# Scores of both RWKV heads of a chunk by one matmul with 256 moving columns, masked in pieces of two chunks

## The chip, the cores and the metric

The kernel runs on one core of a Trainium2 chip. The metric is the time of one execution on the device in microseconds, the median of a few runs. Five engines with queues of their own work in parallel: PE (matmul; its weight loads are listed apart as PEld), DVE (vector), ACT (activation), POOL, and SP, which here only issues DMAs. Each engine executes its own list of instructions strictly in order, and an instruction that waits for a semaphore holds up all that stand behind it on that engine.

## The reference, cut to what matters

The program is one decoder layer for a sequence of 1024 positions at model width 1024: a mixer with three head groups (a gated unit, a linear recurrence, and six heads of RWKV-7 time mixing), and a gated feed-forward. The change touches only the RWKV-7 part:

```python
def step(state, inp):
    r_t, w_t, k_t, v_t, kk_t, a_t = inp
    sa = jnp.einsum('bhvk,bhk->bhv', state, kk_t)
    state = (state * w_t[:, :, None, :]
             - sa[..., :, None] * (kk_t * a_t)[..., None, :]
             + v_t[..., :, None] * k_t[..., None, :])
    return state, jnp.einsum('bhvk,bhk->bhv', state, r_t)
...
_, out = lax.scan(step, state0, tuple(seq_first))
```

The kernel computes this recurrence in chunks of 64 positions. Within a chunk it needs the products of every position's two queries (`kk` and `r`, scaled by the accumulated decay) with every position's two keys (`kk*a` and `k`), cut by a causal mask. These products are the scores.

## The kernel before, in words

The sequence is worked in two halves of 512 positions (f = 0 and 1), and the six heads in three pairs (j = 0, 1, 2). One call of `rwkv(j, f)` does a pair for a half; such a call is a unit below, named by its two digits, so unit 21 is j=2 of the second half. A unit has eight chunks in two groups g of four, and its pair of heads hh lies on the 128 partitions as 64 and 64.

`KB` holds the keys, [128, chunk, 2, 64]: for each chunk a stationary operand of 128 columns. `KG[g]` holds the queries, [128, chunk, 2, 128]: it is block-diagonal over the heads, so the 64 columns of head hh are zero on the partitions of the other head. The score matmuls take a chunk's `KB` as weights and, for each head, the 2x64 columns of that head in `KG` as the moving operand: 128 columns, eight matmuls for a group, four into each of two `pg` tiles (one for each head). Two DVE operations then mask each `pg`: line 633 writes the upper 64 rows times `mr` into `AK`, and line 635 writes the lower 64 rows times a causal mask into `SC`. `pg` comes from the PSUM pool `mp` with three buffers, which almost all small products of the mixer share.

What follows from them: `AK` goes to DRAM and comes back in other shapes (lines 642 to 687) for the triangular inverse, of which `lanes()` does one half on DVE (lines 678 and 680, fifteen small steps) and `chain()` the other on PE (line 695, tiles `pz`, `py`). Then `chain()` runs over the eight chunks one after the other: each step is a few matmuls (line 748, tile `q`), a copy `Y` on ACT, again a matmul, `U` on DVE (line 760), the new state `SS` on DVE (line 766), so it is a round trip over three engines; every step waits for the state of the one before. `finish()` normalises the result (lines 777 to 799). The names in these stages carry the unit: `q_217` is chunk 7 of unit 21.

The stages are generators, and the string `ORDER` says in which order they are advanced when the program is built (P is a unit's start, L its lanes, M with two digits its chain, E its finish, and R, B, U belong to the other groups). That order is only a priority: within each engine the instructions are then ordered when the program is built, by expected durations and dependencies, unless they are pinned. So an operation of another length moves its neighbours, all through the mixer. The large products (lines 251 to 253, three matmuls of 512 columns for each of eight row blocks, because each operand is split into a high part and a low part) stand between the small ones. Their low weights `wl_...` are made on DVE (line 234). After the mixer come the output projection (`po`, line 1036) and the feed-forward, from about 600 us on.

Of the kernel before, what the change touches and what calls it, by code (L numbers as in the profile page):

```python
# [10 lines left out]
F32 = mybir.dt.float32  # L11
# [3 lines left out]
ALU = mybir.AluOpType  # L15
# [3 lines left out]
P = 128  # L19
# [135 lines left out]
def trunk(ctx: ExitStack, tc: tile.TileContext, xT, wmod, w_in, w_out, w_up, w_down,  # L155
          par, const, sgu_ln, sgu_wT, sgu_b, lora, g2w, lruw, outT):
    nc = tc.nc
    V, A, G, T = (Ordered(tc, e) for e in (nc.vector, nc.scalar, nc.gpsimd, nc.tensor))
# [18 lines left out]
    m64 = cst[:, C_M64:C_M64 + P]  # L177
# [129 lines left out]
    mp = ctx.enter_context(tc.tile_pool(name="mp", bufs=3, space=PSUM))  # L307
# [182 lines left out]
    for i in range(2):  # L490
        r_, c_ = slice(64 * i, 64 * i + 64), slice(384 * i, 384 * i + 384)
# [26 lines left out]
    mr = r2.tile([P, 8, P], F32, name="mr")  # L518
    G.tensor_copy(mr[:, :, 64:P], m64[:, 64:P].unsqueeze(1).broadcast_to([P, 8, 64]))

    def t2(nm):
        return r2.tile([P, H], F32, tag="t2", name=nm, bufs=NT2)
# [29 lines left out]
    def rwkv(j, f, stages):  # L552
        jc = slice(j * P, (j + 1) * P)
        n = f"{j}{f}"
# [3 lines left out]
        KG, SC, ST = [[t[i] for i in gi] for t in (KGd, SCd, STd)]  # L558
        AK = AKd[turns["p"] % 2]
# [18 lines left out]
        a = t2(f"a{n}")  # L578
# [25 lines left out]
        KB = r2.tile([P, 8, 2, 64], F32, tag="KB", name=f"KB{n}", bufs=2)  # L604
# [17 lines left out]
        eng("rk", "G").tensor_tensor(k, r, k, ALU.mult)  # L622

        for g in range(2):
            pg = [mp.tile([P, 4, 2, 64], F32, tag="m", name=f"pg{n}{g}{hh}") for hh in range(2)]
            for hh in range(2):
                r_ = slice(64 * hh, 64 * hh + 64)
                for c in range(4):
                    T.matmul(pg[hh][:, c, :, :], KB[:, 4 * g + c, :, :].rearrange("p a b -> p (a b)"),  # L629
                             KG[g][:, c, :, r_], start=True, stop=True)  # L630
            for hh in range(2):
                r_ = slice(64 * hh, 64 * hh + 64)
                V.tensor_tensor(AK[r_, 4 * g:4 * g + 4, :, r_], pg[hh][0:64],
                                mr[r_, 4 * g:4 * g + 4, :].rearrange("p c (q t) -> p c q t", q=2), ALU.mult)
                V.tensor_tensor(SC[g][r_, :, :, r_], pg[hh][64:128],
                                m64[64:128, :].rearrange("p (q t) -> p q t", q=2).unsqueeze(1)
                                .broadcast_to([64, 4, 2, 64]), ALU.mult)

        dA = drp.tile([8, 2, 4160], F32, tag="dA", name=f"dA{n}", bufs=3)
        for hh in range(2):  # L640
            r_ = slice(64 * hh, 64 * hh + 64)
# [5 lines left out]
        for g in range(2):  # L647
# [3 lines left out]
            for q in range(2):  # L651
                for hh in range(2):
                    r_ = slice(64 * hh, 64 * hh + 64)
# [330 lines left out]
    for f in range(2):  # L984
        stages[f"X{f}"] = x_in(f)
        for j in range(3):
            stages[f"P{j}{f}"] = rwkv(j, f, stages)
            stages[f"B{j}{f}"] = lru(j, f, stages)
        stages[f"U{f}"] = sgu(f)
    V.on = VPIN > 0  # L990
    for nw, w in enumerate(ORDER.split()):
        if nw == VPIN:
            V.on = False
        n, _, c = w.partition("*")
# [309 lines left out]
    for k in range(KT):  # L1304
        n = (g1 - g0) * P
# [120 lines left out]
```

## Time and profile before

| | |
|---|---|
| median of 3 runs | 1365.76 us (1365.09 to 1372.66) |
| the profiled execution | 1365.03 us |
| its span in the profile | 1362.9 us |
| mean granted TensorE clock | 0.961 of full speed |
| PE, DVE, ACT, POOL busy | 92%, 67%, 43%, 21% of the span |

The span is what the profile covers; 2.1 us of the profiled execution lie outside it. PE is the engine that is busy most, and it is seldom idle for long; where it is, the profile says which instruction it waited for. A share is an average over the whole program: the mixer, to which the change belongs, is the first 570 us.

### The profile page before, as it was taken

How to read it: one execution, taken by the hardware profiler on the slowest of the kernel's cores; microseconds unless marked ns; L12 is line 12 of the kernel's file. 1: busy time of each engine (PE TensorE's matmuls, PEld its weight loads, DVE VectorE, ACT ScalarE, POOL GpSimd, SP SyncE). 2: the span in 40 equal slices, each digit the busy share in tenths (PEclk: the TensorE clock that was granted, in tenths of full speed). 3: DMA queues.
4: the chain of work that ended last, by engine and by line, in shares of the span. 5: the costliest groups of instructions: out<-in, count | busy, mean ns of one | idle time of the engine just before them, and what ended most of it. 6: DMA issues, size and time to landing. Idle time of an engine off the chain costs nothing. (4 is left out here: it accounts for less than half of the span.)

```text
span 1362.9 us, 18607 instructions
## 1 busy us (share of the span) xinstructions
PE 1248.6 (92%) x6948; PEld 1021.3 (75%) x6948; DVE 913.0 (67%) x1703; ACT 583.0 (43%) x1008; POOL 289.2 (21%) x258
## 2 busy tenths in 40 slices
PE   3769999879998989789988899999999999999996
PEld 3557878667786867668867788888888888888885
DVE  6878776777778586567797666666656675332566
ACT  5365554665663367234453334343343342111231
POOL 6652221304123100000002433333233200000000
PEclk9889999889999889889988899999999999999998
DMA  7444151443315144585232222222222373321213
GB/s 288 153 140 135 41 162 53 130 128 90 100 40 153 32 115 144 175 271 168 86 84 92 87 85 93 75 73 93 85 93 66 128 256 123 92 86 43 82 55 124
DMA packets 87498, 153.88 MB, mean 113 GB/s; under 512 B 37617, under 2 KB 39281, under 8 KB 87409
## 3 DMA queue, kind: packets, MB, share of 16 engines
q1 hardware_dynamic: 87264, 152.45, 35.6%
q8 instruction: 54, 0.88, 0.3%
q14 instruction: 36, 0.29, 0.1%
q10 hardware_dynamic: 144, 0.26, 0.1%
HBM read 126.60 MB, written 26.08 MB: 112 GB/s over the span
## 5 line engine op out<-in xcount | busy, mean ns | idle before, releaser
L1266 DVE SCALAR_TENSOR_TENSOR x<-pd,modc,x 128x512 f32<-128x512 f32 x80 | 59.6, 749 | 83.7 <-PE pd L253 83.7
L292 POOL TENSOR_TENSOR macc<-macc,wm 128x512 f32<-128x512 f32 x35 | 54.3, 1551 | 95.1 <-ACT wm L290 90.3
L233 ACT CAST wh_wd<-wr_wd 128x768 fp32r<-128x768 f32 (+2 forms) x32 | 21.7, 677 | 96.5 <-PE pd L252 94.2
L1207 POOL TENSOR_TENSOR wr_uv<-wr_uv 128x512 f32<-128x512 f32 x3 | 5.7, 1910 | 233.3 <-DVE wr_ub L1206 233.3
L234 DVE TENSOR_TENSOR wl_ug<-wr_ug,wh_ug 128x1024 fp32r<-128x1024 f32 x22 | 29.1, 1323 | 36.9 <-ACT wh_ug L233 36.6
L1315 POOL TENSOR_TENSOR x<-x,rb_n 128x512 f32<-128x512 f32 x2 | 3.0, 1516 | 218.5 <-ACT rb_n L275 218.5
L1244 POOL TENSOR_TENSOR u<-u,g 128x512 f32<-128x512 f32 x21 | 27.7, 1320 | 99.6 <-ACT g L1155 99.6
L233 ACT CAST wh_ug<-wr_ug 128x1024 fp32r<-128x1024 f32 x22 | 23.2, 1054 | 40.6 <-PE pA L1130 32.7
L1223 DVE TENSOR_TENSOR p<-p,pB 128x512 f32<-128x512 f32 x21 | 14.4, 686 | 32.8 <-PE pB L1131 30.4
L748 PE MATMUL q<-SS,KGd 128*128 128x64 f32 x180 | 35.6, 281 | 0.0
L768 ACT COPY O<-q 128x64 f32<-128x64 f32 x48 | 10.1, 210 | 58.3 <-PE q L748 58.2
L629 PE MATMUL pg<-KGd,KB 128*128 128x128 f32 x192 | 29.4, 300 | 5.4 <-DVE KGd L614 5.4
L748 PE MATMUL q<-VV,SCd 128*128 128x64 f32 x192 | 32.8, 278 | 1.4 <-ACT VV L662 0.8
L1148 DVE SCALAR_TENSOR_TENSOR g<-pA,pr,g 128x511 f32<-128x511 f32 (+1 forms) x42 | 31.2, 744 | 3.6 <-ACT g L1146 3.5
L748 PEld LDWEIGHTS q<-VV,SCd 128*128 128x128 f32 x192 | 28.5, 196 | 5.7 <-ACT VV L662 1.6
L1148 DVE SCALAR_TENSOR_TENSOR g<-p,pr,g 128x511 f32<-128x511 f32 (+1 forms) x42 | 32.1, 765 | 0.5 <-ACT g L1146 0.4
L1155 ACT ACTIVATE g<-g 128x512 f32<-128x512 f32 x44 | 27.9, 634 | 9.8 <-DVE g L1150 9.8
L290 ACT ACTIVATE wm<-wm,cs 128x512 f32<-128x512 f32 x35 | 24.5, 721 | 17.6 <-DMA wm<-in_wmod_dram 17.5
L760 DVE TENSOR_SCALAR U<-q,rn 128x64 f32<-128x64 f32 x48 | 13.5, 280 | 27.6 <-PE q L748 21.5
L629 PEld LDWEIGHTS pg<-KGd,KB 128*128 128x128 f32 x192 | 26.3, 209 | 6.2 <-DVE KGd L614 5.9
L233 ACT CAST wh_wo<-wr_wo 128x1024 fp32r<-128x1024 f32 x16 | 16.7, 1049 | 31.3 <-PE po L252 16.2
L1209 POOL TENSOR_TENSOR wr_ug<-wr_ug,wr_uv 128x512 f32<-128x512 f32 x18 | 28.9, 1604 | 1.4
(5029 smaller groups left out, 4415.0 us busy)
## 6 DMA issues: line engine op xcount, KB each, us to landing
wm<-in_wmod_dram SPq DMA_DIRECT2D x48, 512.0 KB, 4.6
wr_ug<-in_w_up_dram SPq DMA_DIRECT2D x22, 512.0 KB, 3.7
wr_uv<-in_w_up_dram SPq DMA_DIRECT2D x22, 512.0 KB, 3.6
wr_g<-gd SPq DMA_DIRECT2D x22, 512.0 KB, 3.5
x<-in_xT_dram SPq DMA_DIRECT2D x32, 256.0 KB, 4.8
wr_wo<-in_w_out_dram SPq DMA_DIRECT2D x16, 512.0 KB, 4.6
wr_wd<-in_w_down_dram SPq DMA_DIRECT2D x16, 384.0 KB, 3.1
gd<-c SPq DMA_DIRECT2D x21, 256.0 KB, 2.0
```

The lines of the kernel that those rows point to most:

```text
L233: A.copy(hi, src)
L234: (e or V).tensor_tensor(lo, src, hi.bitcast(F32), ALU.subtract)
L290: A.activation(acc if k == 0 else wt[:, j, :], wt[:, j, :], AF.Copy, scale=cs[:, k:k + 1])
L292: G.tensor_tensor(acc, acc, wt[:, j, :], ALU.add)
L629: T.matmul(pg[hh][:, c, :, :], KB[:, 4 * g + c, :, :].rearrange("p a b -> p (a b)"), KG[g][:, c, :, r_], start=True, stop=True)
L748: T.matmul(o, w, x, start=start, stop=True, skip_group_check=True)
L1148: V.scalar_tensor_tensor(g[:, d:H], src[:, 0:H - d], taps[2 - d], g[:, d:H], ALU.mult, ALU.add)
L1155: A.activation(g, g, AF.Silu)
L1209: eng("S4" + e, "G").tensor_tensor(g1, g1, v1, ALU.subtract)
L1223: V.tensor_tensor(self.p1, self.p1, psB, ALU.add)
L1244: eng("c22", "V").tensor_tensor(u3, u3, g1_, ALU.mult)
L1266: V.scalar_tensor_tensor(x, ps, modc[:, 40 + k:41 + k], x, ALU.mult, ALU.add)
```

## The change

Both heads of a chunk are now scored by one matmul: `KG[g][:, c, :, :]` is the moving operand, all 256 columns, so a group has four matmuls instead of eight. A `pg` tile holds two chunks with both heads instead of four chunks with one; its size is the same, and there are still two for a group. A mask operation reads one head's columns of two chunks, so a group has eight operations of 64x256 elements instead of four of 64x512.

```diff
--- before.py
+++ after.py
@@ -622,19 +622,19 @@
         eng("rk", "G").tensor_tensor(k, r, k, ALU.mult)
 
         for g in range(2):
-            pg = [mp.tile([P, 4, 2, 64], F32, tag="m", name=f"pg{n}{g}{hh}") for hh in range(2)]
-            for hh in range(2):
-                r_ = slice(64 * hh, 64 * hh + 64)
-                for c in range(4):
-                    T.matmul(pg[hh][:, c, :, :], KB[:, 4 * g + c, :, :].rearrange("p a b -> p (a b)"),
-                             KG[g][:, c, :, r_], start=True, stop=True)
-            for hh in range(2):
-                r_ = slice(64 * hh, 64 * hh + 64)
-                V.tensor_tensor(AK[r_, 4 * g:4 * g + 4, :, r_], pg[hh][0:64],
-                                mr[r_, 4 * g:4 * g + 4, :].rearrange("p c (q t) -> p c q t", q=2), ALU.mult)
-                V.tensor_tensor(SC[g][r_, :, :, r_], pg[hh][64:128],
-                                m64[64:128, :].rearrange("p (q t) -> p q t", q=2).unsqueeze(1)
-                                .broadcast_to([64, 4, 2, 64]), ALU.mult)
+            pg = [mp.tile([P, 2, 2, P], F32, tag="m", name=f"pg{n}{g}{i}") for i in range(2)]
+            for c in range(4):
+                T.matmul(pg[c // 2][:, c % 2, :, :], KB[:, 4 * g + c, :, :].rearrange("p a b -> p (a b)"),
+                         KG[g][:, c, :, :], start=True, stop=True)
+            for i in range(2):
+                cg = slice(4 * g + 2 * i, 4 * g + 2 * i + 2)
+                for hh in range(2):
+                    r_ = slice(64 * hh, 64 * hh + 64)
+                    V.tensor_tensor(AK[r_, cg, :, r_], pg[i][0:64, :, :, r_],
+                                    mr[r_, cg, :].rearrange("p c (q t) -> p c q t", q=2), ALU.mult)
+                    V.tensor_tensor(SC[g][r_, 2 * i:2 * i + 2, :, r_], pg[i][64:128, :, :, r_],
+                                    m64[64:128, :].rearrange("p (q t) -> p q t", q=2).unsqueeze(1)
+                                    .broadcast_to([64, 2, 2, 64]), ALU.mult)
 
         dA = drp.tile([8, 2, 4160], F32, tag="dA", name=f"dA{n}", bufs=3)
         for hh in range(2):
```

The matmuls with tile `pg` fall from 96 to 48 and the masks rise from 48 to 96; all else is the same work. The order on the engines changes through the mixer, down to the first rows of the output projection; the feed-forward's order is unchanged. Three places follow.

DVE, in unit 20, ahead of `wl_yg20`, the low weights of the gate product of R20 (`LX20`, `LT20` are the steps of unit 20's lanes, `rsq_o10` belongs to the finish of unit 10, `ig10` and `xr10` to the linear recurrence). Before:

```order
L680 TENSOR_TENSOR LX20_2219<-LX20_2219,LT20_2220 128x4x8
L225 TENSOR_TENSOR rsq_o10_2269<-rsq_o10_2269 128x8
L816 SCALAR_TENSOR_TENSOR xr20_2346<-pb20_2321,pr_66,xr20_2346 128x509
L678 TENSOR_TENSOR LT20_2220<-LX20_2219,LA20_2218 128x35
L226 SCALAR_TENSOR_TENSOR rsq_o10_2269<-rsq_o10_2269 128x8
L845 TENSOR_TENSOR ig10_1666<-ig10_1666,xr10_1659 128x512
L680 TENSOR_TENSOR LX20_2219<-LX20_2219,LT20_2220 128x5x7
L224 TENSOR_TENSOR rsq_o10_2269<-rsq_o10_2269 128x8
L846 SCALAR_TENSOR_TENSOR xr10_1659<-rg10_1665,ig10_1666 128x512
L678 TENSOR_TENSOR LT20_2220<-LX20_2219,LA20_2218 128x30
L225 TENSOR_TENSOR rsq_o10_2269<-rsq_o10_2269 128x8
L234 TENSOR_TENSOR wl_yg20_2421<-wr_yg20_2420,wh_yg20_2422 128x1024
```

After:

```order
L838 SCALAR_TENSOR_TENSOR rg10_1665<-ig10_1666,rg10_1665 128x512
L678 TENSOR_TENSOR LT20_2220<-LX20_2219,LA20_2218 128x14
L782 TENSOR_SCALAR mv10_2261<-mv10_2261 128x8
L840 SCALAR_TENSOR_TENSOR ig10_1666<-rg10_1665 128x512
L680 TENSOR_TENSOR LX20_2219<-LX20_2219,LT20_2220 128x14
L220 TENSOR_SCALAR rsq_o10_2269<-mv10_2261 128x8
L222 TENSOR_SCALAR rsq_o10_2269<-mv10_2261 128x8
L678 TENSOR_TENSOR LT20_2220<-LX20_2219,LA20_2218 128x26
L221 TENSOR_SCALAR rsq_o10_2269<-rsq_o10_2269 128x8
L234 TENSOR_TENSOR wl_yg20_2421<-wr_yg20_2420,wh_yg20_2422 128x1024
```

`wl_yg20` now stands ahead of `ig10` and `xr10` (845, 846) and of seven pairs of lane steps.

PE, at the start of unit 11's chain over the chunks (`q_110`, `q_111`), with `pb21`, a large product of the linear recurrence. Before:

```order
L253 MATMUL pb21_4514<-h14h_2658,wl_xr21_4509 128x512
L748 MATMUL q_110_4066<-Y110_4067,AKd0_121 128x64
L748 MATMUL q_110_4066<-SS_98,KGd2_114 128x64
L251 MATMUL pb21_4514<-h15h_2665,wh_xr21_4510 128x512
L252 MATMUL pb21_4514<-h15l_2666,wh_xr21_4510 128x512
L253 MATMUL pb21_4514<-h15h_2665,wl_xr21_4509 128x512
L748 MATMUL q_110_4066<-U110_4068,STd2_120 128x64
L251 MATMUL pb21_4514<-h16h_2672,wh_xr21_4510 128x512
L252 MATMUL pb21_4514<-h16l_2673,wh_xr21_4510 128x512
L253 MATMUL pb21_4514<-h16h_2672,wl_xr21_4509 128x512
L748 MATMUL q_110_4066<-U110_4068,AKd0_121 128x64
L748 MATMUL q_111_4081<-SS_98,KGd2_114 128x64
```

After:

```order
L253 MATMUL pb21_4514<-h17h_2679,wl_xr21_4509 128x512
L748 MATMUL q_110_4066<-Y110_4067,AKd0_121 128x64
L748 MATMUL q_110_4066<-SS_98,KGd2_114 128x64
L748 MATMUL q_110_4066<-U110_4068,STd2_120 128x64
L748 MATMUL q_110_4066<-U110_4068,AKd0_121 128x64
L748 MATMUL q_111_4081<-SS_98,KGd2_114 128x64
L748 MATMUL q_112_4096<-VV11_3407,SCd2_117 128x64
L748 MATMUL q_111_4081<-Y111_4082,AKd0_121 128x64
```

The large matmuls of `pb21` that stood inside the chain's first steps now stand ahead of the chain.

PE, at the end of the last chain, unit 21, and ahead of its finish (`po21`); `po02` is the third tile of the output projection. Before, from the chain's last matmul on (three more rows of `po02` and then `po21` follow):

```order
L748 MATMUL q_217_4919<-U217_4921,AKd1_122 128x64
L252 MATMUL po02_5151<-y03l_5045,wh_wo02_5147 128x512
L253 MATMUL po02_5151<-y03h_5044,wl_wo02_5146 128x512
L251 MATMUL po02_5151<-y04h_5050,wh_wo02_5147 128x512
L252 MATMUL po02_5151<-y04l_5051,wh_wo02_5147 128x512
L253 MATMUL po02_5151<-y04h_5050,wl_wo02_5146 128x512
L251 MATMUL po02_5151<-y05h_5054,wh_wo02_5147 128x512
L252 MATMUL po02_5151<-y05l_5055,wh_wo02_5147 128x512
L253 MATMUL po02_5151<-y05h_5054,wl_wo02_5146 128x512
L251 MATMUL po02_5151<-y06h_5060,wh_wo02_5147 128x512
L252 MATMUL po02_5151<-y06l_5061,wh_wo02_5147 128x512
L253 MATMUL po02_5151<-y06h_5060,wl_wo02_5146 128x512
```

After:

```order
L748 MATMUL q_217_4919<-U217_4921,AKd1_122 128x64
L251 MATMUL po02_5151<-y07h_5064,wh_wo02_5147 128x512
L252 MATMUL po02_5151<-y07l_5065,wh_wo02_5147 128x512
L253 MATMUL po02_5151<-y07h_5064,wl_wo02_5146 128x512
L788 MATMUL po21_5002<-ident_68,O21_4127 128x128 x4
L798 MATMUL pgt21_5013<-sgg1_2685,g2s_517 128x512
```

Of the rows of `po02`, 14 stood between the chain's last matmul and `po21`; now three do.

## Rows read from the trace of the kernel before

**Rows 1.** Windows: stretch, length, busy PE, PEld, DVE, ACT, POOL; clock; DMA.

```profile
240.00:290.00 50.00, 37.02 (x326) 27.03 (x326) 37.95 (x90) 37.48 (x63) 12.23 (x10) 0.86 0.52 148
...
440.00:490.00 50.00, 49.10 (x449) 41.53 (x449) 29.84 (x62) 21.13 (x51) 5.40 (x5) 0.90 0.23 57
...
670.00:1180.00 510.00, 497.09 (x2145) 406.93 (x2144) 337.45 (x502) 198.45 (x322) 133.29 (x96) 0.98 0.32 101
```

**Rows 2.** Instructions of tile pg: durations min/median/max in ns, first and last start.

```profile
L629 PE MATMUL pg<-KGd,KB x192: 270/275/582, 90.5 to 478.8; 128*128 128x128 f32 x192
L633 DVE TENSOR_TENSOR AKd<-pg,mr x24: 672/683/685, 92.7 to 480.5; 64x512 f32<-64x512 f32 x24
L635 DVE TENSOR_TENSOR SCd<-pg,cst x24: 692/694/697, 93.4 to 481.2; 64x512 f32<-64x512 f32 x24
```

**Rows 3.** PE timeline: start, length of the run, line, form, count.

```profile
458.87 0.61 PE L748 MATMUL q<-VV,SCd 128*128 128x64 f32 x4
...
477.26 1.78 PE L629 MATMUL pg<-KGd,KB 128*128 128x128 f32 x14
...
486.41 1.08 PE L827 MATMUL pra<-xr,lrw 128*128 128x512 f32 x2
487.33 1.02 PE L830 MATMUL pix<-xr,lrw 128*128 128x512 f32 x2
```

**Rows 4.** DVE operations on 256 elements and lane steps L678, columns as in rows 2.

```profile
L614 DVE TENSOR_TENSOR KGd<-r,gm x24: 407/423/1494, 89.0 to 473.5; 64x256 f32<-64x256 f32 x24
...
L678 DVE TENSOR_TENSOR LT<-LX,LA x90: 155/182/1300, 111.1 to 507.3; 128x30 f32<-128x30 f32 x18, 128x14 f32<-128x14 f32 x12, 128x24 f32<-128x24 f32 x12, 128x15 f32<-128x15 f32 x6
...
L900 DVE TENSOR_SCALAR sv<-pzt,smv,rsq_a x8: 535/540/543, 130.6 to 423.8; 128x256 f32<-128x256 f32 x8
```

**Rows 5.** DVE timeline: start, length; unit 20's stretch; unit 21's first and last mask.

```profile
249.49 0.68 DVE L777 TENSOR_REDUCE mv<-O 128x8 f32<-128x512 f32 x1
...
260.40 0.68 DVE L845 TENSOR_TENSOR ig<-ig,xr 128x512 f32<-128x512 f32 x1
...
261.19 1.22 DVE L846 TENSOR_TENSOR_SCAN xr<-rg,ig 128x512 f32<-128x512 f32 x1
...
262.48 1.22 DVE L234 TENSOR_TENSOR wl_yg<-wr_yg,wh_yg 128x1024 fp32r<-128x1024 f32 x1
...
476.02 0.68 DVE L633 TENSOR_TENSOR AKd<-pg,mr 64x512 f32<-64x512 f32 x1
...
481.23 0.69 DVE L635 TENSOR_TENSOR SCd<-pg,cst 64x512 f32<-64x512 f32 x1
```

**Rows 6.** PE timeline, the longest waits of the mixer; in brackets idle before, releaser.

```profile
263.75 0.80 PE L253 MATMUL pyg<-h00h,wl_yg 128*128 128x512 f32 x1 [5.79 <-DVE wl_yg L234]
...
280.21 1.05 PE L695 MATMUL pz<-X,AKd 16*32 16x16 f32 x64 [5.04 <-DVE X L700]
...
282.87 0.79 PE L251 MATMUL pc_xwa<-h10h,wh_xwa 128*128 128x512 f32 x1 [0.39 <-ACT h10h L329]
...
498.79 0.79 PE L253 MATMUL pu<-h10h,wl_u 128*128 128x512 f32 x1 [5.43 <-DVE wl_u L234]
```

**Rows 7.** Chain that ended last: start, share of one large matmul, line.

```profile
757.36 0.43 PE pD L1130
...
761.32 0.23 PE pC L1129
```

**Rows 8.** PE timeline, unit 11's chain: Y of chunks 0, 1 and 2.

```profile
455.29 0.33 PE L748 MATMUL q<-Y,AKd 128*128 128x64 f32 x2
...
458.48 0.33 PE L748 MATMUL q<-Y,AKd 128*128 128x64 f32 x2
...
461.62 0.39 PE L748 MATMUL q<-Y,AKd 128*128 128x64 f32 x2
```

**Rows 9.** PE timeline, end of the last chain and start of its finish.

```profile
555.58 0.33 PE L748 MATMUL q<-U,AKd 128*128 128x64 f32 x2
...
563.49 1.12 PE L788 MATMUL po<-ident,O 128*128 128x128 f32 x4 [4.31 <-DVE O L785]
```

## The prediction

> **What bounds the kernel now.** I read the page's busy shares first, which stand in the table above: PE 92%, DVE 67%. Matmul records overlap, so a busy PE is not yet a full one. The windows by stage come next [rows 1]. In the feed-forward (670 to 1180 us) PE is busy 497 of 510 us, and the change leaves that order alone, so nothing is won or lost there. The mixer is uneven: from 240 to 290 us PE is busy only 37 of 50 us at a clock of 0.86, while DVE is busy 38; from 440 to 490 us PE is busy 49 and DVE 30. So PE's work sets the pace in most of the mixer, and for the rest it is what PE waits for. The waits of over 5 us [rows 6] are three: at 263.75 us for `wl_yg`, at 280.21 us for `X` and at 498.79 us for `wl_u`. All three were released by DVE. So a saving on PE counts almost in full, an added wait behind DVE counts, and DVE's own time counts only where PE waits for it. A large matmul of 512 columns takes 0.43 us of the chain that ended last in one place and 0.23 us in another [rows 7]; those are TensorE's two levels, 1.2 and 2.4 GHz, and a stretch with long waits runs partly at the lower one, as the clock of 0.86 says.
>
> **Part 1, the matmuls on PE: about nothing.** A matmul on f32 data is two instructions in the trace, so 96 matmuls are 192 instructions [rows 2]. Their duration (275 ns) holds the pipeline's length; what counts is the spacing. The run of 14 takes 1.78 us in all, so a spacing is (1.78 - 0.275)/13 = 0.116 us [rows 3]. For 64 columns the run of four gives (0.61 - 0.275)/3 = 0.112 us [rows 3], the same, so below 128 columns something else than columns sets the spacing. For 512 columns, two instructions start 487.33 - 486.41 = 0.92 us before the next pair, or 0.46 us each [rows 3]. Between 0.116 us at 128 and 0.46 us at 512, a straight line gives 0.116 + 128 x 0.344/384 = 0.231 us at 256. A group then costs 8 x 0.231 = 1.85 us, where it was 16 x 0.116 = 1.86 us. So 128 columns are just the width at which the columns begin to count, and halving the number of matmuls gives nothing back. The lower bound is a 256-column instruction at the price of a 128-column one: 8 x 0.116 = 0.93 us saved for each of 12 groups, 11.1 us. I take the line, since its two ends are this kernel's own f32 matmuls, and book 0 us.
>
> The Trainium skill ("TensorE: Matmul & The Clock Gate", section "Back-to-back issue gap") speaks for the lower end: in a stream of weight loads and matmuls it gives about 81 ns for a matmul at 128 columns and 131 ns at 512. By that a group would fall from 16 x 81 = 1.30 us to at most 8 x 131 = 1.05 us, as an estimate from that page at least 3 us over the 12 groups. The trace disagrees with its size here: 0.46 us against 0.116 us is a ratio of 4, not 1.6.
>
> **Part 2, the masks on DVE: 8.6 us more work, of which I book 2.9.** Eight masks of a unit stand in sequence; in unit 21 the first starts at 476.02 us and the last at 481.23 us [rows 5], with one small operation between; their mean duration is 0.689 us [rows 2] and with the step between two it is about 0.72 us, so 8 x 0.72 = 5.8 us. There will be 16 masks of 256 elements. No row shows such a mask from PSUM. The nearest are the `KG` products, a tensor-tensor operation with 64x256 elements, 0.423 us, and line 900, which reads 256 elements from PSUM but takes two scalars by pointer, 0.540 us [rows 4]. With 0.03 us between two, the 16 take 7.2 us or 9.1 us, so a unit pays 1.4 us or 3.4 us more. Nothing makes it less than the fastest `KG` product, 0.407 us [rows 4], or 1.2 us for a unit; a gain is excluded, because the elements are the same and the operations are twice as many. I take 0.423 us, since the mask is the same kind of operation with the same shape. Six units give 8.6 us. Behind the masks stand, on DVE, the chain's `U` and `SS`, which PE waits for, and low weights. In stretches like 440 to 490 us DVE is idle for 40% [rows 1] and the delay is absorbed there; where DVE is already late [rows 6] all of it shows. I book a third, 2.9 us; the bounds are 0 and 8.6 us. The masks can also begin no earlier: the first two chunks cost PE 4 x 0.231 = 0.92 us, as the first head's four did (8 x 0.116). The DMA of `AK` follows the last masks and so is up to 1.4 us later; in the unit of [rows 6] it meets `X`, which is counted with the next part.
>
> **Part 3, the order of the neighbours: about +1 us.** Three places from the order, priced by rows.
>
> Place 1, `wl_yg20` [rows 5, 6]. From L777 at 249.49 us to the end of `wl_yg` at 262.48 + 1.22 = 263.70 us DVE needs 14.2 us. In the new order 845, 846 and seven pairs of lane steps stand behind it: 845 takes 0.68 us, 846 1.22 us [rows 5], and a lane step 0.18 us by the median of L678 [rows 4], so seven pairs 2.5 us; together 4.4 us. So the wait of 5.79 us may shrink to about 1 us, and the matmuls behind it may keep their full clock: 13 of them at 0.23 instead of 0.43 us [rows 7], 2.6 us. That is 7 us at best. Against it, the finish of unit 10 (`po10`) still needs those DVE steps, and the `h` tiles of the second half, the first of which PE takes at 282.87 us [rows 6], wait for DVE and ACT work that stands behind the finish; also the masks come later. I book -3 us, bounds -7 and 0.
>
> Place 2, unit 11's chain [rows 8]. A step over a chunk takes 458.48 - 455.29 = 3.2 us with nine large matmuls inside and 461.62 - 458.48 = 3.1 us without: it is a round trip, and the large matmuls ride in it free. Nine of them now stand ahead of the chain, at 0.23 us each [rows 7]: +2.1 us, bounds 0 (the chain may have waited anyway) and 3.
>
> Place 3, the end of the mixer [rows 9]. From the chain's last matmul at 555.58 us to `po21` at 563.49 us there are 7.9 us of round trip, of which 4.31 us are idle and 14 large matmuls fill most of the rest. Eleven of these 14 now stand ahead of the chain's end, 11 x 0.23 = 2.5 us less cover; low weights that stood inside the finish on DVE now stand where DVE waits for ACT, which I put at about 0.7 us back. I book +1.8 us, bounds 0 and 2.5.
>
> The wait at 498.79 us stays: the rows of the recurrence that leave its front are matched by large matmuls that left PE's side.
>
> **Sum.** 0 + 2.9 - 3 + 2.1 + 1.8 = +3.8 us on the profiled execution of 1365.03 us, so 1368.8 us. That execution lies 0.7 us below the median of 1365.76 us. I forecast 1369 us: no difference to speak of, a shade slower. About 1%, 13.7 us, is what a measurement of this kernel can tell from no change.
>
> **Rivals.**
>
> *Wide matmuls are cheap or place 1 pays in full.* If 256 columns cost PE what 128 do, 11.1 us go: 1358 us. If place 1 gives its 7 us and the masks stay hidden, -7 + 2.1 + 1.8 = -3.1: 1362 us. For it: PE waits little otherwise, so what is saved there counts. Against it: the 512-column rows [rows 3], and the work behind place 1. Chance 0.2 for both; only both together, with places 2 and 3 absorbed (1365 - 11.1 - 7 = 1347 us), pass 1%.
>
> *The masks are dear and DVE becomes the bound.* If 256 elements from PSUM with a strided read cost what line 900 does [rows 4], a unit pays 3.4 us, and if every unit's delay lands in front of low weights or `U` that PE waits for, as in [rows 6], that is 20 us, and with places 1 to 3 at +0.9 us the time is 1387 us. It decides from a mask of about 0.50 us: 16 x 0.53 - 5.8 = 2.7 us for a unit, 16 us in all. For it: the waits over 5 us are all behind DVE. Against: DVE is idle 40% of a stretch with masks. Chance 0.09.
>
> *The matmuls are not what the change moves at all.* PE and DVE both absorb it and the new order evens out: 1365 to 1366 us. It lies inside the forecast's range.
>
> **How the numbers follow.** The forecast with its neighbourhood (1364 to 1375 us) has 0.6, the first rival 0.2, the second 0.09, and what I have not traced in the new order, such as other neighbours moved by a few us either way, the rest. The terms' own bounds, without the rivals, reach from -7 us to 8.6 + 3 + 2.5 = +14.1 us, 1359 to 1380 us beside the median, and that is the range; it takes in most of the first rival and leaves out the second. Faster by over 1%: 0.03. Within 1%: 0.88. Slower by over 1%: 0.09.
>
> **What would show it.** In the new profile: 96 matmul instructions for `pg` at a spacing of 0.21 to 0.24 us; 96 masks at 0.41 to 0.43 us; DVE's busy time up by about 6 to 9 us, PE's sum nearly unchanged; the wait for `wl_yg` much shorter than 5.79 us, with a longer wait soon after it; a longer wait at `po21` than 4.31 us; the stretch after 670 us as long as before. The forecast is wrong if the spacing at 256 columns is nearer 0.12 us, if a mask takes over 0.5 us, or if a wait of several us appears at a place that I did not look at.

## The result and the profile after

The changed kernel takes 1389.85 us (median of 4 runs, 1387.82 to 1394.44); the kernel before took 1368.33 us on the same chip (4 runs, 1365.09 to 1372.66). The ratio is 1.0173 [1.0147, 1.0199]: 1.7% slower, where 1369 us with a range of 1359 to 1380 us was forecast. The profiled execution took 1394.44 us with a span of 1392.3 us. It is the slowest of its four, and the profile of before (1365.03 us) lies below all four runs of its kernel, so the two traces lie 29 us apart where the medians lie 21.5 us apart. Differences between traces are read with that in mind, and ratios of many runs decide.

These are the page's busy shares, first of before, then of the changed kernel:

```profile
PE 1248.6 (92%) x6948; PEld 1021.3 (75%) x6948; DVE 913.0 (67%) x1703; ACT 583.0 (43%) x1008; POOL 289.2 (21%) x258
...
PE 1270.8 (91%) x6852; PEld 1031.7 (74%) x6852; DVE 918.0 (66%) x1751; ACT 585.8 (42%) x1009; POOL 281.9 (20%) x258
```

DVE is busy only 5 us longer. PE is busy 22.2 us longer with 96 instructions fewer, and idle 7.2 us longer (its span less its busy time, 121.5 us against 114.3): most of the 29 us is PE taking longer over its own instructions, at a mean granted clock of 0.942 where it was 0.961. Whether that clock is the cause is asked below. Next the tile `pg` after, in the columns of [rows 2]:

```profile
L627 PE MATMUL pg<-KGd,KB x96: 379/380/793, 90.9 to 495.1; 128*128 128x256 f32 x96
L633 DVE TENSOR_TENSOR AKd<-pg,mr x48: 403/417/419, 93.1 to 498.6; 64x256 f32<-64x256 f32 x48
L635 DVE TENSOR_TENSOR SCd<-pg,cst x48: 425/427/429, 93.5 to 499.1; 64x256 f32<-64x256 f32 x48
```

And one group on PE's timeline (start, length of the run), four wide matmuls in eight instructions:

```profile
162.76 1.95 PE L627 MATMUL pg<-KGd,KB 128*128 128x256 f32 x8
```

The eight run in 1.95 us, so a spacing is (1.95 - 0.38)/7 = 0.224 us, against 0.231 us on the prediction's straight line between 128 and 512 columns. A group of sixteen narrow ones cost 16 x 0.116 = 1.86 us, one of eight wide ones 8 x 0.224 = 1.79 us. The masks take 0.417 and 0.427 us, against 0.423 us. The operations that the change touches cost what was forecast. By the Trainium skill ("TensorE: Matmul & The Clock Gate", section "Back-to-back issue gap") the eight would take at most 8 x 131 = 1050 ns, an estimate from its figure for 512 columns; by this row these f32 instructions of 256 columns are dearer.

Now the windows by stage that answer to [rows 1], with the end of the mixer as a fourth (500 to 600 us; the last line is the same stretch before):

```profile
240.00:290.00 50.00, 39.25 (x177) 29.12 (x176) 38.53 (x98) 37.53 (x60) 12.15 (x10) 0.88 0.55 156
440.00:490.00 50.00, 45.65 (x370) 37.56 (x368) 28.03 (x68) 15.07 (x31) 7.27 (x6) 0.80 0.22 68
500.00:600.00 100.00, 83.30 (x553) 63.39 (x551) 55.16 (x142) 52.60 (x93) 0.00 (x0) 0.80 0.38 115
670.00:1180.00 510.00, 496.29 (x2156) 406.53 (x2156) 345.12 (x522) 203.67 (x328) 133.26 (x96) 0.98 0.32 102
...
500.00:600.00 100.00, 87.47 (x592) 68.34 (x591) 63.34 (x129) 46.57 (x80) 0.00 (x0) 0.89 0.57 184
```

The feed-forward (670 to 1180 us) is as before. From 440 to 490 us PE is busy 45.65 us at a clock of 0.80, where it was 49.10 us at 0.90. From 500 to 600 us the clock is 0.80; it was 0.89. The new order is late by then, so these two stretches do not hold quite the same instructions as before. The loss lies in the mixer. In a kernel below that has the new order alone, equal instructions are late by some 7 us at 200 us, 12 us at 350, 16 us at 460 to 500 and 23 us from 600 on.

PE's waits between 60 and 690 us, by who ended them (us in total, times, longest):

```profile
PE po L788 <- DVE O L785: 6.7, 2, 6.1
PE pc_xwa L251 <- ACT h10h L329: 5.3, 1, 5.3
PE pu L251 <- ACT wh_u L233: 4.9, 1, 4.9
...
PE po L788 <- DVE LX L680: 3.0, 1, 3.0
...
PE pyg L253 <- DVE wl_yg L234: 1.0, 1, 1.0
```

Of the long waits of [rows 6] the one for `wl_yg` shrank from 5.79 to 1.0 us as forecast, and others took its place within 20 us: `po10` waits 3.0 us and `pc_xwa` 5.3 us for `h10h`. The wait of 5.04 us for `X` is gone. `po21` waits 6.1 us where it waited 4.31 us [rows 9]. But PE's idle time in this stretch, 630 us less its busy time, is 65.4 us by the windows, against 60.3 us before. Five microseconds of waits don't make 21.

### The profile page after: what moved, and what is told of

It is laid out like the page before. It is cut to its first block, busy times and chain, and to the rows that moved or that the text cites. A ratio compares the mean times of both kernels' runs of the same rounds, so it can differ in the third digit from the quotient of the medians.

```text
span 1392.3 us, 18461 instructions
## 1 busy us (share of the span) xinstructions
PE 1270.8 (91%) x6852; PEld 1031.7 (74%) x6852; DVE 918.0 (66%) x1751; ACT 585.8 (42%) x1009; POOL 281.9 (20%) x258
## 5 line engine op out<-in xcount | busy, mean ns | idle before, releaser
L292 POOL TENSOR_TENSOR macc<-macc,wm 128x512 f32<-128x512 f32 x35 | 49.4, 1413 | 76.4 <-ACT wm L290 66.0
L1244 POOL TENSOR_TENSOR u<-u,g 128x512 f32<-128x512 f32 x21 | 27.7, 1320 | 99.1 <-ACT g L1155 99.1
L233 ACT CAST wh_ug<-wr_ug 128x1024 fp32r<-128x1024 f32 x22 | 23.1, 1050 | 40.7 <-PE pA L1130 32.7
L627 PE MATMUL pg<-KGd,KB 128*128 128x256 f32 x96 | 32.1, 466 | 7.1 <-DVE KGd L614 7.1
L748 PE MATMUL q<-SS,KGd 128*128 128x64 f32 x180 | 38.6, 300 | 0.0
L748 PEld LDWEIGHTS q<-SS,KGd 128*128 128x128 f32 x180 | 31.1, 216 | 0.1
```

What stands on the lines that cost most here:

```text
L233: A.copy(hi, src)
L292: G.tensor_tensor(acc, acc, wt[:, j, :], ALU.add)
L627: T.matmul(pg[c // 2][:, c % 2, :, :], KB[:, 4 * g + c, :, :].rearrange("p a b -> p (a b)"), KG[g][:, c, :, :], start=True, stop=True)
L748: T.matmul(o, w, x, start=start, stop=True, skip_group_check=True)
```

## The experiments

### Work or order

The change does two things at once: it alters 144 operations, and it makes the build put all instructions of the mixer in another order. These kernels separate the two. Each carries a table that fixes the order of every engine's instructions, by edges that force an order and add no wait:

```diff
+PINNED = {"PE": "0-111 120-130 112-115 ...", "DVE": ..., "Activation": ..., "Pool": ..., "SP": ...}
+def pin(tc):
+    ...
+        for p, q in zip(rank, rank[1:]):
+            tc.add_manual_dep(ins[q], ins[p].name, mybir.DependencyInfo(
+                mybir.DependencyClass.NoSync, mybir.DependencyReason.DATA), reason="pin")
```

`new_work_old_order` has the changed matmuls and masks in the order of before.

> The changed kernel with every engine's instructions held in the order of the kernel before: four wide matmuls stand where the eight narrow ones stood (each in the place of the second of a pair), two half masks where one mask stood; nothing else differs. Theory A (the loss of 24 us comes from the new order of the neighbours, through waits and TensorE's half clock): 1362 to 1373 us, within 5 us of the kernel before, and the stretches at half clock as before. Theory B (the doubled masks on DVE make it late): 1380 to 1392 us. Theory C (the wide matmuls themselves are slow or let the clock fall): 1380 to 1392 us too; the run half_masks_old_order tells B from C.

Measured: 1370.28 us, ratio 0.9988 [0.9968, 1.0008].

`old_work_new_order` has the matmuls and masks of before in the changed kernel's order.

> The kernel before with every engine's instructions held in the order of the changed kernel: eight narrow matmuls stand where four wide ones stood, one mask where two half masks stood. Theory A (new order): 1382 to 1394 us, as slow as the changed kernel, with the long stretch at half clock near 540 to 570 us. Theories B and C (new work): 1360 to 1372 us.

Measured: 1392.76 us, ratio 1.0151 [1.0118, 1.0185].

`half_masks_old_order` has the narrow matmuls and the sixteen half masks, in the order of before:

```diff
             for c in range(4):
-                T.matmul(pg[c // 2][:, c % 2, :, :], KB[...], KG[g][:, c, :, :], ...)
+                for hh in range(2):
+                    r_ = slice(64 * hh, 64 * hh + 64)
+                    T.matmul(pg[c // 2][:, c % 2, :, r_], KB[...], KG[g][:, c, :, r_], ...)
```

> Narrow matmuls as before (eight in a group, 128 columns), written into tiles of two chunks, and 16 half masks in a unit as in the changed kernel, all in the order of the kernel before. Theory A: within 5 us of the kernel before, and DVE's busy time up by about 8 us. Theory B (masks): 1380 to 1392 us. Theory C (wide matmuls): as the kernel before. Its difference from new_work_old_order is the price of the matmuls' width: 0 by the prediction's line between 128 and 512 columns, -11 us by the lower bound.

Measured: 1371.18 us, ratio 1.0007 [0.9984, 1.0030].

`changed_again` is the changed kernel itself, beside the three.

> The changed kernel on the same chip as the three others, for comparison: 1386 to 1394 us, 1.5 to 2.0% over the kernel before, by every theory.

Measured: 1393.19 us, ratio 1.0147 [1.0115, 1.0179].

What follows: the order alone, with none of the changed work, costs all of it, 1.51% of 1370 us or 20.7 us. The table that fixes an order adds nothing: `changed_again` has none and takes 1.0147. The changed work in the old order costs nothing that can be measured. Between the first and the third, wide against narrow matmuls is 0.9988 against 1.0007, some 2.6 us in the wide ones' favour, less than the intervals tell; the sixteen half masks cost 1 us at 1.0007, also within them.

### Is it the half clock behind the waits?

In the new order PE's mean clock from 60 to 690 us is 0.91, before 0.94. One theory was that the waits themselves cost little, but drop TensorE to its lower level (1.2 GHz) for what follows. Zero matmuls of 512 columns, which add nothing to the sums, were put into the waits.

`new_order_waits_filled` is the changed kernel with 23 of them in six waits:

```diff
+COVER = {"pz10": 2, "po10": 3, "pc_xwa1": 5, "pu01": 5, "pz21": 2, "po21": 6}
+    def cover(ps, n, first=True):
+        zero = m64[:, 0:1].broadcast_to([P, H])
+        for _ in range(n):
+            T.matmul(ps, ident, zero, start=first, stop=False, skip_group_check=True)
```

> The changed kernel in its own order, with 23 extra matmuls of zeros (512 columns, f32, about 0.92 us each at full clock, 21 us together) put on TensorE directly ahead of six of its waits: 2 ahead of pz10, 3 ahead of po10, 5 ahead of the first of pc_xwa1, 5 ahead of pu01, 2 ahead of pz21, 6 ahead of po21. They add zeros or are overwritten. Theory A1 (the waits are short; what costs is the half clock that follows them): 1370 to 1383 us against about 1391 without them, and the time at half clock up to 660 us falls from 116 to 135 us to under 100. Theory A2 (the round trips behind DVE and ACT themselves make the loss, the clock follows from something else): 1387 to 1396 us, as without them or a little more.

Measured: 1387.62 us, ratio 1.0140 [1.0116, 1.0165].

`old_order_waits_filled` has the changed work in the order of before, with 20 of them in four of its five longest waits (`pz20`, `po21`, `pyg20`, `pu01`).

> The new work in the order of the kernel before, with 20 extra matmuls of zeros inside its own four longest waits: 6 at wl_yg20 and 5 at wl_u01 (in the middle of their groups), 5 ahead of pz20, 4 ahead of po21. Without them this kernel took 0.9988 of the kernel before. A1: 0.990 to 0.996 of the kernel before, because the stretches at half clock after 262, 280 and 497 us go. A2: 0.998 to 1.003.

Measured: 1370.07 us, ratio 1.0026 [1.0011, 1.0041].

The windows from 60 to 690 us, of the changed kernel run again and then with its waits filled:

```profile
60.00:690.00 630.00, 566.70 (x3801) 450.94 (x3801) 442.16 (x1029) 323.04 (x587) 109.23 (x124) 0.91 0.40 119
...
60.00:690.00 630.00, 580.61 (x3881) 456.77 (x3880) 445.23 (x1037) 326.99 (x595) 107.69 (x123) 0.94 0.39 118
```

The clock came back to 0.94, the level of before (over the whole program the mean is 0.954 to 0.960 in the six runs of this kernel and 0.943 to 0.948 in those of `changed_again`), and the time did not follow: 1.0140 against 1.0147. That alone decides little, because the zero matmuls are work of PE too: 23 x 0.92 = 21 us, an estimate from the f32 pair of 512 columns in [rows 3]. Their price could hide a gain from the clock. The starts of equal instructions speak against that. These are the first of `pc_xwa` and that of `po21`, each without and with the fill (the filled kernel's lines are numbered a little higher):

```profile
291.90 0.80 PE L251 MATMUL pc_xwa<-h10h,wh_xwa 128*128 128x512 f32 x1 [5.33 <-ACT h10h L329]
...
284.03 0.50 PE L259 MATMUL pc_xwa<-h10h,wh_xwa 128*128 128x512 f32 x1 [1.70 <-ACT h10h L339]
...
591.99 1.11 PE L788 MATMUL po<-ident,O 128*128 128x128 f32 x4 [6.08 <-DVE O L785]
...
584.61 0.66 PE L800 MATMUL po<-ident,O 128*128 128x128 f32 x4 [0.90 <-DVE O L796]
```

The filled kernel's trace, the fastest of its six and from another chip, lies 4.6 us ahead of the other just before its first zero matmul, and some 3 us come on behind that fill, at `pz10`. From there the lead stays: 7.7 us before the fill at `po10`, 7.9 us at `pc_xwa`, 7.4 us at `po21` and 7.8 us behind it. In between it gained 1.6 us behind `pu01` and lost 1.4 at `pz21`. As the cause of the whole loss the theory falls: behind five of the six waits the faster PE gains nothing that lasts, because it waits again for DVE and ACT (behind `pc_xwa` 1.6 us for `h10l`, where it was 0.9). At `pz21` the fill did not keep the clock up, and what the half clock costs there is seen below. In the order of before the same filling made nothing faster: 1.0026 [1.0011, 1.0041], where the same kernel without it had 0.9988.

### Where in the program

Here the order is changed over from one to the other at a point of time, on all five engines at once; what had started by then in the trace stands in the first order, the rest in the second. All have the work of before.

`new_to_305`: the new order up to 305 us.

> The work of the kernel before; every engine follows the new order as far as it had come at 305 us of the run old_work_new_order, and the old order from there. If the loss is the sum of independent places, what the new order had lost by then stays and nothing is added: 8 to 12 us over the kernel before, 1376 to 1382 us. If one late place makes the loss (pz21 with the half clock after 541 us): within 4 us of the kernel before. If a delay early on starts all the later ones: 1385 us or more.

Measured: 1376.44 us, ratio 1.0066 [1.0043, 1.0088]. In its trace `wl_u`'s matmul, at 498.79 us before [rows 6], starts at 512.65 us:

```profile
512.65 0.80 PE L253 MATMUL pu<-h10h,wl_u 128*128 128x512 f32 x1 [5.42 <-DVE wl_u L234]
```

Equal instructions from 300 to 580 us, by the median of every 20 us, are late by the same 13.8 to 14.0 us: what was lost ahead of the change-over is neither made up nor enlarged behind it. Some 3 us come back at the end of the mixer.

`old_to_500`: the order of before up to 500 us, then the new one.

> The work of the kernel before; the old order as far as it had come at 500 us of the kernel before, the new one from there. Sum of independent places: 4 to 9 us over the kernel before (the shift grows from 17 to 23 us behind 500 us in old_work_new_order). If one late place makes the whole loss: 18 to 24 us over. If the late loss only follows from an early delay: within 3 us.

Measured: 1375.85 us, ratio 1.0057 [1.0035, 1.0079].

`new_to_500`: the new order up to 500 us, then that of before.

> The work of the kernel before; the new order as far as it had come at 500 us of old_work_new_order, the old order from there: the counterpart of old_to_500, which lost 0.0057. If the stretches add, this one loses the rest of the 0.0151, 0.008 to 0.011 (1377 to 1382 us beside 1367); new_to_305 had 0.0066 of it. If the end of the mixer absorbs what was lost before: under 0.006. If the late loss needs the early one: over 0.012.

Measured: 1382.27 us, ratio 1.0111 [1.0089, 1.0134].

The stretches have 0.66% up to 305 us, 1.11 - 0.66 = 0.45% from there to 500 us, and 1.51 - 1.11 = 0.40% behind 500 us. These three add up to 1.51% by the way they are reckoned; what tests it is the last stretch taken alone, 0.57% [0.35, 0.79], which agrees with 0.40% within the intervals. So no single place holds it all.

### Single instructions put back

The next kernels take the new order with the work of before and put back what looked like the cause at one place each.

`sqrt_back`: at unit 00 the new order puts a square root, which brings two loads of ACT's function tables with it, ahead of the copies `Z` in the inverse. It goes back to where it stood:

```diff
 L233 CAST wh_u_1553<-wr_u_1551 128x1024
-L843 ACT_TABLE_LOAD
-L843 ACTIVATE ig_878<-ig_878 128x512
 L725 COPY Z_1020<-py_1097 32x256
```

> The kernel before in the new order (1.0151 of the kernel before), with two instructions put back: ScalarE's square root on ig00 (line 843) stands behind unit 10's sg and gm again, ahead of line 844, and VectorE's line 845 directly ahead of line 846. In the new order the square root stood ahead of unit 00's Z and unit 10's sg and brought two table loads of 1.28 us with it: 3.2 us for sg, and the first U of unit 00 stands behind it on VectorE. Theory D (single instructions on the path of a unit's chain, each place by itself): first U of unit 00 3 us earlier, 1.012 to 1.0135 of the kernel before. Theory E (the mixer absorbs a single place, the loss is of the order as a whole): 1.0145 to 1.0165.

Measured: 1388.65 us, ratio 1.0168 [1.0143, 1.0193].

`la_ahead`: unit 01's load of `LA` goes ahead of a load of `wm` in SP's queue.

```diff
 L642 DMA dA_2954<-AKd_122 64x8x64 x2
+L673 DMA LA_3059<-dA_2954 64x16x16 x2
 L286 DMA wm_3_3590<-in_wmod_dram 128x1024
-L673 DMA LA_3059<-dA_2954 64x16x16 x2
```

> The new order with the load of LA01 put ahead of the load of wm7_3 in SyncE's queue again, and ScalarE's square for unit 20's finish (osq20) ahead of its scaling of wm7_3. In the new order wm7_3 waited for a buffer until 354.8 us and LA01 behind it came at 355.6 us, 8 us behind the last mask of unit 01 instead of 3 us. D: unit 01's lane steps begin 4 us earlier, 1.011 to 1.013. E: 1.0145 to 1.0165.

Measured: 1385.65 us, ratio 1.0156 [1.0124, 1.0187].

`lanes_ahead`: in unit 21 the last lane steps go ahead of `o11` and its neighbours on DVE, `X` ahead of the low halves `y00l` to `y05l`, and `pz21` back between the large matmuls of `pyg21` on PE.

```diff
 L678 TENSOR_TENSOR LT_4416<-LX_4415,LA_4414 128x24
-L796 TENSOR_TENSOR o_4498<-o_4498,bv_3409 128x512
 L680 TENSOR_TENSOR LX_4415<-LX_4415,LT_4416 128x6x4
...
+L700 STREAM_TRANSPOSE X_4642<-AKd_122 32x256 x4
 L234 TENSOR_TENSOR y00l<-yr_5028,y00h 128x512
```

> The new order with unit 21's way to its chain put back: VectorE's last eight lane steps ahead of the product o11 (line 796, which waits for ScalarE) and its four transposes X121 ahead of the y lows, ScalarE's Z21 and AKd1 copies among the y casts, TensorE's pz21 in two groups ahead of the last nine and the last six matmuls of pyg21. D: first U of unit 21 5 to 6 us earlier, no half clock of 10 us and more behind 541 us, 1.010 to 1.012. E: 1.0145 to 1.0165.

Measured: 1390.6 us, ratio 1.0177 [1.0150, 1.0205].

`three_back`: all three.

> All three repairs together. D: 3 + 4 + 5.5 us less than the new order, 1.005 to 1.008 of the kernel before. E: 1.013 to 1.0165. In between: the places overlap.

Measured: 1398.91 us, ratio 1.0233 [1.0205, 1.0261].

None gave anything back, and the three together cost more than the new order alone. The traces told why the obvious edit missed its place: in `lanes_ahead` the lanes' result was ready at 523.1 us, but its DMA started at 527.13 us, behind others in SP's queue. So these followed, which mend more engines at the same places.

`unit00_back`: `sqrt_back`, and the second group of `py00` on PE back ahead of eight large matmuls.

> As sqrt_back, and TensorE's second group of py00 also stands ahead of eight large matmuls of pc_v10 again, as in the old order: all three engines on unit 00's way to its chain are put back, not ScalarE and VectorE alone (there the first U of unit 00 came only 1 us earlier, since TensorE reached py00 no sooner). Theory F (a place is worth its microseconds only if every engine and queue on the way is put back): first U of unit 00 at about 145 us, 3 us earlier, 1.012 to 1.0135 of the kernel before. Theory E (a single place is absorbed by the next one): 1.0145 to 1.017.

Measured: 1387.35 us, ratio 1.0147 [1.0123, 1.0171].

`unit21_back`: `lanes_ahead`, and SP's queue at that place as before.

> As lanes_ahead, and SyncE's queue is put back too: the two stores of LX21 ahead of the store of xr11, the two loads of AKd1 between the stores of o11 and ya01, yr02 behind them. In lanes_ahead the store of LX21 waited 4 us in the queue behind yr02 and gave the 4.6 us gain of the lane steps back. F: X121 at about 530 us instead of 534 to 536, first U of unit 21 5 to 6 us earlier, 1.010 to 1.012. E: 1.0145 to 1.017.

Measured: 1388.57 us, ratio 1.0158 [1.0128, 1.0188].

`units_back`: both.

> unit00_back and unit21_back together. F: 8 to 9 us less than the new order, 1.0075 to 1.010. E: 1.013 to 1.017.

Measured: 1392.28 us, ratio 1.0189 [1.0163, 1.0215].

Again nothing. In `unit21_back` `pz21` no longer waits, but the first `U` of unit 21 still comes only at 554.63 us. Ahead of the next step, `py`, PE now waits for the weights of the output projection, which ACT and DVE make behind the `y` halves:

```profile
542.88 0.50 PE L251 MATMUL po<-y00h,wh_wo 128*128 128x512 f32 x1 [4.66 <-ACT wh_wo L233]
```

Here a place mended by hand passed its gain on to the next instruction that was still in the new order.

### One place exchanged whole

The last two take the change-over in time again, now at both ends of one place: all that the order has between about 500 us and the first chain step of unit 21, on all five engines. The core of the edit on PE (before is -, the new order +; `wo` are the weights of the output projection):

```diff
-L695 MATMUL pz_4648<-X_4642,AKd_122 32x16 x32
 L251 MATMUL pyg_4941<-h15h,wh_yg_4937 128x512
 L252 MATMUL pyg_4941<-h15l,wh_yg_4937 128x512
 L253 MATMUL pyg_4941<-h15h,wl_yg_4936 128x512
-L695 MATMUL pz_4648<-AKd_122,Z_4643 16x16 x32
...
-L695 MATMUL py_4720<-X_4642,AKd_122 32x32 x16
...
+L695 MATMUL pz_4648<-X_4642,AKd_122 32x16 x32
+L695 MATMUL pz_4648<-AKd_122,Z_4643 16x16 x32
 L251 MATMUL po_5076<-y00h,wh_wo_5072 128x512
...
+L695 MATMUL py_4720<-X_4642,AKd_122 32x32 x16
```

`only_unit21`: the order of before everywhere, the new one at this place alone.

> Work of before. Its order of before on every engine except one place: the instructions that the new order puts between about 500 us and unit 21's first chain step (U of chunk 0) stand in the new order, all engines together; after them the order of before again. Before, the whole new order after 500 us alone cost 0.57%. If the place around unit 21's lanes, its pz and py groups and the first weights of the output projection carries that stretch's loss: 1.004 to 1.006 of the kernel before, some 6 to 8 us. If the loss is of the order as a whole, and a single place's delay is taken up at the next wait: 0.999 to 1.002.

Measured: 1375.46 us, ratio 1.0068 [1.0042, 1.0094].

`all_but_unit21`: the new order everywhere but at this place.

> The counterpart: work of before in the new order everywhere, except that the instructions between about 500 us and unit 21's first chain step stand in the order of before, all engines together. The new order up to 500 us with the order of before behind it gave 1.0111, the new order throughout 1.0151. If the place carries the last stretch's loss: 1.010 to 1.012. If the delay comes back at the next wait, as it did in the repairs of single instructions: 1.014 to 1.017.

Measured: 1379.65 us, ratio 1.0100 [1.0081, 1.0118].

Both ways the place carries the loss of its stretch: 0.68% or 9.3 us put in, 1.51 - 1.00 = 0.5% or 7 us taken out; the intervals of 1.0151 and 1.0100 meet only at their ends, at 1.0118. The rows show how. The first PE row of `wl_u` (498.79 us before) is a mark ahead of the place, and the first `U` of unit 21 one behind it. Before, rows of PE (the small matmuls `pz`, `py` with large ones between them) and the first two `U` on DVE:

```profile
518.45 0.72 PE L695 MATMUL pz<-X,AKd 16*32 16x16 f32 x64 [0.16 <-PE pyg L253]
519.10 0.50 PE L251 MATMUL pyg<-h15h,wh_yg 128*128 128x512 f32 x1
...
522.38 0.69 PE L695 MATMUL py<-X,AKd 32*32 32x32 f32 x32
...
528.69 0.28 DVE L760 TENSOR_SCALAR U<-q,rn 128x64 f32<-128x64 f32 x1 [2.46 <-PE q L748]
533.60 0.28 DVE L760 TENSOR_SCALAR U<-q,rn 128x64 f32<-128x64 f32 x1 [1.76 <-PE q L748]
```

The same of `only_unit21`:

```profile
503.77 0.80 PE L253 MATMUL pu<-h10h,wl_u 128*128 128x512 f32 x1 [5.42 <-DVE wl_u L234]
...
525.70 0.72 PE L695 MATMUL pz<-X,AKd 16*32 16x16 f32 x64 [1.65 <-DVE X L700]
526.89 0.69 PE L695 MATMUL pz<-AKd,Z 32*16 32x16 f32 x64 [0.48 <-ACT Z L707]
528.61 0.80 PE L251 MATMUL po<-y00h,wh_wo 128*128 128x512 f32 x1 [1.03 <-ACT wh_wo L233]
...
531.44 1.07 PE L695 MATMUL py<-X,AKd 32*32 32x32 f32 x32
...
540.93 0.28 DVE L760 TENSOR_SCALAR U<-q,rn 128x64 f32<-128x64 f32 x1 [9.05 <-PE q L748]
549.89 0.28 DVE L760 TENSOR_SCALAR U<-q,rn 128x64 f32<-128x64 f32 x1 [3.90 <-PE q L748]
```

And of `all_but_unit21`:

```profile
514.53 0.79 PE L253 MATMUL pu<-h10h,wl_u 128*128 128x512 f32 x1 [5.68 <-DVE wl_u L234]
...
533.97 0.72 PE L695 MATMUL pz<-X,AKd 16*32 16x16 f32 x64 [0.16 <-PE pyg L253]
...
544.21 0.28 DVE L760 TENSOR_SCALAR U<-q,rn 128x64 f32<-128x64 f32 x1 [2.46 <-PE q L748]
```

From the mark to the first `U` it is 29.9 us before, 29.7 us in `all_but_unit21`, and 37.2 us in `only_unit21` (37.2 us in `old_work_new_order` too). Of these 7.3 us, 4.1 have been lost when `py` starts (522.38 - 498.79 = 23.6 us behind the mark before, 531.44 - 503.77 = 27.7 now): `pz` waits for `X`, which stands behind six `y` halves on DVE, and `py` stands behind five large matmuls of the output projection, the first of which waits for its weights. The other 3.2 us are lost between `py` and `U` (6.3 us before, 9.5 now; 8.5 in `old_work_new_order`), and there PE waits for nothing and has fewer large matmuls than before, seven instead of ten. The windows of `only_unit21` show what it is:

```profile
510.00:520.00 10.00, 10.00 (x56) 8.02 (x55) 6.46 (x19) 5.36 (x8) 0.00 (x0) 1.00 0.58 192
520.00:530.00 10.00, 6.81 (x149) 4.87 (x147) 8.30 (x14) 6.78 (x14) 0.00 (x0) 0.88 0.66 207
530.00:540.00 10.00, 10.00 (x81) 5.51 (x82) 1.81 (x3) 6.46 (x10) 0.00 (x0) 0.50 0.42 138
540.00:550.00 10.00, 10.00 (x42) 8.43 (x42) 2.90 (x8) 3.06 (x6) 0.00 (x0) 0.50 0.07 26
```

From 524 to 529 us PE has only the small `pz` matmuls and three waits, so that it is busy 6.81 of the 10 us; then the granted clock is 0.50, the lower of the two levels, while PE is busy all the time. Before, with `pyg` between the small matmuls, the same stretch ran at 1.00:

```profile
520.00:530.00 10.00, 9.88 (x168) 6.41 (x167) 5.75 (x10) 9.48 (x18) 0.00 (x0) 1.00 0.70 220
530.00:540.00 10.00, 9.62 (x63) 8.58 (x64) 3.94 (x11) 7.45 (x13) 0.00 (x0) 1.00 0.07 27
```

How long the half clock lasts differs between runs. In `only_unit21` and the profiled run of the changed kernel it is 15.6 and 16.3 us from the first to the third `U`, in `old_work_new_order` and `changed_again` 9.9 us, before 9.5 us: another 6 us, in some profiles. The profile of `only_unit21` is the slowest of its six runs, so the traced loss of this kernel is larger than its median shows.

## Why the prediction was wrong, point by point

**What bounds the kernel: one wait was missed.** The waits of over 5 us were four, not three. The fourth stands directly ahead of the first changed matmuls:

```profile
90.50 5.18 PE L629 MATMUL pg<-KGd,KB 128*128 128x128 f32 x24 [5.21 <-DVE KGd L614]
```

After the change it is 6.6 us; nothing in the sum hung on it.

**Part 1, the matmuls: right.** The spacing is 0.224 us against 0.231, and the changed work in the old order measures 0.9988.

**Part 2, the masks: right in price; how much of it shows is too little to tell.** A mask takes 0.417 to 0.427 us against 0.423. Of the 8.6 us, 2.9 were booked as showing; the half masks alone measure 1.0007, about 1 us, and 0 and 2.9 both lie in the interval.

**Part 3, the order of the neighbours, is the step that failed.** It was entered at about +1 us, from three places priced one by one, with every other neighbour that the new order moves put at nothing and no row to say why. It is +20.7 us. None of the three places brings that, nor all of them. Place 1 happened as described: the wait for `wl_yg` went from 5.79 to 1.0 us. It returned nothing that lasts, since the next instructions of the finish (`po10`, 3.0 us) and the `h` tiles (`h10h`, 5.3 us) came late, the very counter-argument that was named and then booked at less than the gain. The wait for `X`, which part 2 passed on to this part, was priced nowhere; it went away. Place 2 was booked at 2.1 us with a bound of 3; from the first to the last `U` of unit 11's chain the traces show 30.8 us before (456.01 to 486.83 us) and 35.6 us after (468.46 to 504.04 us), 4.8 us more:

```profile
456.01 0.26 DVE L760 TENSOR_SCALAR U<-q,rn 128x64 f32<-128x64 f32 x1
...
486.83 0.28 DVE L760 TENSOR_SCALAR U<-q,rn 128x64 f32<-128x64 f32 x1
...
468.46 0.26 DVE L760 TENSOR_SCALAR U<-q,rn 128x64 f32<-128x64 f32 x1
...
504.04 0.28 DVE L760 TENSOR_SCALAR U<-q,rn 128x64 f32<-128x64 f32 x1
```

Place 3's wait came, 6.1 us against 4.31, but from the last `U` to `po21` it is 7.6 us after (588.20 to 595.84 us) and was 8.6 us (554.86 to 563.49 us), so it gave 1 us back where 1.8 us were booked against it:

```profile
554.86 0.28 DVE L760 TENSOR_SCALAR U<-q,rn 128x64 f32<-128x64 f32 x1 [0.32 <-PE q L748]
...
588.20 0.28 DVE L760 TENSOR_SCALAR U<-q,rn 128x64 f32<-128x64 f32 x1 [1.95 <-PE q L748]
...
595.84 1.12 PE L788 MATMUL po<-ident,O 128*128 128x128 f32 x4 [6.09 <-DVE O L785]
```

What the step lacked is that the new order differs all through the mixer. The places were chosen from the differences that looked large beside known waits, and the rest was left at zero on balance, with a few microseconds either way. The runs show a loss in every stretch instead, 0.66, 0.45 and 0.40 to 0.57%. One place was found and priced from both sides, unit 21's at 7 to 9 us, a third of the loss or a little more; the prediction did not look at it, and its own last line had named that as what would make it wrong. There the large matmuls of `pyg21` that stood between the small `pz` and `py` matmuls now stand ahead of them, and the work on DVE and ACT that PE needs next stands later.

**The rivals.** Wide matmuls are not cheap (0.224 us is not 0.116), and place 1 did not pay. The dear masks would have given 1387 us, near what was measured, but by the runs the masks cost nothing that can be measured: a right number from a wrong mechanism. "The new order evens out" is refuted.

**What stays open.** More than half of the loss is located only by stretch, not by place. That single repairs returned nothing is shown; that each was taken up by the next misplaced instruction was seen in the rows of unit 21 and is argued for the others. Why the order of before suits the chip better was not tried. No version beat the kernel before; the changed work in its order is its equal.

## What to carry to other kernels

Where a build orders instructions by expected durations, a change of an operation's length is a change of the whole order, and the order can matter far more than the operation: here 20.7 us against nothing that could be measured. Run the new work in the old order and the old work in the new before anything is said of either. Price such a reordering by stretches, exchanged on all engines at once, and not by the places that catch the eye; putting back one instruction tells little. At the place found here the small matmuls of a latency-bound step wanted large ones between them, which filled PE's waits and kept its clock for what follows.

## What the runs showed of the hardware

The half clock is costly or free by what follows. Raising the mean clock from 0.91 to 0.94 with zero matmuls in six waits gave 0.07%, less than can be measured, and equal instructions kept their distance behind five of the six; in unit 21, where PE has ten microseconds of gapless work behind the small matmuls, it costs 2 to 3 us between `py` and the first `U`, and some 6 us more behind it in some profiles. The two zero matmuls ahead of `pz21` did not prevent it: in that kernel the window from 540 to 550 us has PE busy 10.00 us at a clock of 0.61.

This kernel, its order fixed, kept a delay exactly: behind the change-over at 305 us equal instructions stayed 13.8 to 14.0 us late for 280 us on PE, DVE and ACT, until the output projection took up 3 us of it.
